# Two activation tiles begin 160 bytes off the grid of 512 bytes

## The chip, the core and the metric

The kernel runs on one core of one Trainium2 chip. The time is the device time of one execution in microseconds (us). A core has a matrix engine (TensorE, "PE" in the profile, its weight loads "PEld"), a vector engine (VectorE, "DVE"), a scalar engine (ScalarE, "ACT"), GpSimd ("POOL") and a queue engine that issues most of the transfers (SyncE, "SP"). All of them work on an on-chip memory of 128 partitions, in which a tile has the same byte address in each partition. TensorE multiplies two operands: one is loaded into the array as weights (128 x 128), the other is streamed through it, up to 512 columns at a time; the result is summed up in accumulator banks.

## The reference, cut to what matters

A trunk of two layers on 256 positions of width 2048. Both layers project their input, run a main branch and a four-head attention over 256 memory positions, gate both, project the result with `w_out`, and normalise.

```
h = x
for i in range(2):
    if i == 1:
        k_blocks, v_blocks, k_mean = moba_shared_kv(h, w_kv_shared)
    u = h @ w_in[i]                       # 2048 -> 4096 columns
    branch_in, gate_b, mem_q, gate_m = split(u)
    branch = multiscale_pool(...) if i == 0 else moba_attention(...)
    mem_o = memory_attention(mem_q, mem, w_mem_kv[i])
    mixed = concatenate([branch * silu(gate_b), mem_o * silu(gate_m)])
    h = layer_norm(ALPHA * h + mixed @ w_out[i], ln_g[i], ln_b[i])
```

All arithmetic is float32. Most of the work is the products of the 256 positions with the weights `w_in`, `w_out`, `w_mem_kv` and `w_kv_shared`.

## The kernel before, in words

To keep float32 accuracy at the fast matmul format, each operand is held as two tiles, a high part and a low part (`split`, L62 to L65: ScalarE writes the rounded high part, VectorE the difference), and a product is three terms: high by high, high by low, low by high. The activations lie transposed in three large tiles: `xT` (the input of a layer), `memT` (the memory) and `zT` (the gated branches), each with 16 k-blocks of 512 columns, 256 of the high part and 256 of the low part. Weights come in blocks of 128 x 1024 (512 KB): a transfer into one of four `raw` buffers, then a split into one of four pairs `wh`, `wl`. The blocks make one list, `items`; `run` walks it and prepares three blocks ahead, so the order of all engines is written out by the list and by `later`, which puts follow-up work some items behind. Nothing is planned by cost.

Two helpers consume the blocks. `proj_t` has the weights as the loaded side and streams xT or memT: for each 128 x 128 piece, the high weights meet all 512 columns of a k-block (high and low of the activation), and the low weights meet the 256 columns of the high part. So 512-wide and 256-wide matmuls alternate in pairs, and two accumulator halves are added at the end (`fold`). A list of 4 blocks has 16 k-blocks by two pieces, 32 pairs. `proj_n` has the activations as the loaded side (xT, memT or zT) and streams 512 columns of the weights: three 512-wide matmuls for each k-block and half of the positions. `proj_t` makes keys, queries, gates and the pooling input; `proj_n` makes values and the output projections.

The second layer's output projection is read in four column blocks. The last is "kept": its weights are split not into the four buffers but into xT and memT, which nobody reads any more, and are multiplied at the very end by `last`, with zT as the loaded side and the kept weights streamed. In the built program, xT begins at byte 1152 of a partition, memT at 33920, zT at 66688, the `raw` buffers at 115840, `wh` at 132224 and `wl` at 148608: all are 128 more than a multiple of 512, and all slices that matmuls take from them are whole multiples of 512 bytes further.

Of the kernel before, what the change touches and what calls it, by code (L numbers as in the profile page):

```python
# [12 lines left out]
F32R = mybir.dt.float32r  # L13
# [4 lines left out]
P = 128  # L18
T = 256
D = 2048  # L20
KT = D // P
# [10 lines left out]

BLK = 1024
RAW_BUFS = 4
W_BUFS = 4
LD = 4
LEAD = 3
LD0 = 8
# [4 lines left out]
def trunk(ctx: ExitStack, tc: tile.TileContext, a: dict, out: bass.AP):  # L43
    nc = tc.nc
    ctx.enter_context(tc.manual_schedule())
    sb = ctx.enter_context(tc.tile_pool(name="sb", bufs=1))
    ps = ctx.enter_context(tc.tile_pool(name="ps", bufs=1, space=bass.MemoryType.PSUM))


    xT = sb.tile([P, KT, 2 * T], F32R, name="xT")  # L50
    memT = sb.tile([P, KT, 2 * T], F32R, name="memT")
    zT = sb.tile([P, KT, 2 * T], F32R, name="zT")
    res = sb.tile([P, 2, D], F32, name="res")
    ident = mask = psc = eps_t = stats = None
# [4 lines left out]
    def mm(o, l, r, start, stop):  # L59
        nc.tensor.matmul(o, l, r, start=start, stop=stop)  # L60
# [9 lines left out]
    def collect(fn, *args):  # L70

        base = len(items)
        fn(*args)
        got = items[base:]
        del items[base:]
        return got

    def item(src, cols, consume=None, dst=None):
        items.append(dict(src=src, cols=cols, consume=consume, dst=dst, cuts=(0, cols)))

    events = defaultdict(list)
    now = [0]
# [4 lines left out]
    def load_piece(it, c0, c1):  # L87
        if "raw" not in it:
            it["raw"] = it.get("land") or sb.tile([P, BLK], F32, name="raw", bufs=RAW_BUFS)
        nc.sync.dma_start(it["raw"][:, c0:c1], it["src"][:, c0:c1])  # L90

    def load(it):
        for c0, c1 in zip(it["cuts"], it["cuts"][1:]):
            load_piece(it, c0, c1)

    def prep_piece(it, c0, c1):
# [7 lines left out]
        if "w" not in it:  # L104
            it["w"] = to or (sb.tile([P, BLK], F32R, name="wh", bufs=W_BUFS),
                             sb.tile([P, BLK], F32R, name="wl", bufs=W_BUFS))
        wh, wl = it["w"]
        split(wh[:, c0:c1], wl[:, c0:c1], raw)

    def prep(it):  # L110
        for c0, c1 in zip(it["cuts"], it["cuts"][1:]):
            prep_piece(it, c0, c1)

    def run():
# [12 lines left out]
        for i in range(n):  # L127
            now[0] = i
            if i + LP < n:
                prep(items[i + LP])  # L130
            if LD0 <= i + LD < n:
                load(items[i + LD])
            it = items[i]
# [14 lines left out]
    def proj_t(mov, wblk, done):  # L148


        acc = []

        def consume(kb):
            def go(wh, wl, k0=0, k1=4):
                if not acc:
                    acc.extend(ps.tile([P, 512], F32, name="acc", bufs=4) for _ in range(2))
                h = wh.rearrange("p (k n) -> p k n", n=256)
                l = wl.rearrange("p (k n) -> p k n", n=256)
                for n in range(2):
                    s = slice(n * P, (n + 1) * P)  # L160
                    for kk in range(k0, k1):
                        k = 4 * kb + kk
                        if k < KT - 1:
                            mm(acc[n], h[:, kk, s], mov[:, k], k == 0, False)
                        mm(acc[n][:, :T], l[:, kk, s], mov[:, k, :T], False, False)
                        if k == KT - 1:
                            mm(acc[n], h[:, kk, s], mov[:, k], False, True)
                    if kb == 3:
                        done(n, acc[n])
            return go  # L170
        for kb in range(4):
            item(wblk[kb], BLK, consume(kb))

    def proj_n(sta, wblk, done, korder=range(8), banks=("acc", "acc")):

        acc = []
        korder = list(korder)

        def consume(j, kb):
            def go(wh, wl):  # L180
                if j == 0:
                    acc.extend(ps.tile([P, 512], F32, name=b, bufs=4 if b == "acc" else 1) for b in banks)
                h = wh.rearrange("p (k n) -> p k n", n=512)
                l = wl.rearrange("p (k n) -> p k n", n=512)
                for t in range(2):
                    for kk in range(2):
                        k = 2 * kb + kk
                        xh = sta[:, k, t * P:(t + 1) * P]
                        xl = sta[:, k, T + t * P:T + (t + 1) * P]
                        first, last = j == 0 and kk == 0, j == 7 and kk == 1  # L190
                        mm(acc[t], xh, h[:, kk], first, False)
                        mm(acc[t], xh, l[:, kk], False, False)
                        mm(acc[t], xl, h[:, kk], False, last)
                    if j == 7:
                        done(t, acc[t])
            return go
        for j, kb in enumerate(korder):
            item(wblk[kb], BLK, consume(j, kb))
# [34 lines left out]
    def heads_tile(name):  # L233
        return sb.tile([P, 4, 2 * T], F32R, name=name)
# [202 lines left out]
    def fresh(key, make):  # L437

        tiles = []

        def g():
            if not tiles:
                tiles.append(make())
                st[key] = tiles[0]
            return tiles[0]
        return g
# [19 lines left out]
    def after(fn):  # L466

        it = items[-1]
        old = it["consume"]

        def go(*w):
            if old is not None:
                old(*w)
            fn()
        it["consume"] = go
# [16 lines left out]
    def load_act(t, src, kb):  # L492
        item(a[src][kb], BLK, None, ("act", t, kb))
# [138 lines left out]
    for grp in range(3):  # L632
        k = fresh("k", lambda: heads_tile("kk"))
# [44 lines left out]
    for j, it in enumerate(collect(out_1)):  # L678
        items.append(it)
        if j == 0:  # L680
            after(load_gb_rows)
        if j >= 8 and j % 2:
            kb = (j - 8) // 2
            w3 = [t[:, 2 * kb:2 * kb + 2].rearrange("p k n -> p (k n)") for t in (xT, memT)]
            item(a["w_out"][1, 3, kb], BLK, None, ("keep", *w3))


# [2 lines left out]
    for i in range(4):  # L690
        items[RAW_BUFS + i]["land"] = scr[:, i * BLK:(i + 1) * BLK]

# [9 lines left out]
    for n in range(4):  # L702
        gb = sb.tile([P, 2, 512], F32, name="raw", bufs=RAW_BUFS)
        for j, nm in enumerate(("ln_g", "ln_b")):
# [3 lines left out]
    def last(t, c0, c1):  # L708
        o = ps.tile([P, 512], F32, name="acc", bufs=4)[:, :c1 - c0]
        for k in range(KT):  # L710
            zh = zT[:, k, t * P:(t + 1) * P]
            zl = zT[:, k, T + t * P:T + (t + 1) * P]
            mm(o, zh, xT[:, k, c0:c1], k == 0, False)
            mm(o, zh, memT[:, k, c0:c1], False, False)
            mm(o, zl, xT[:, k, c0:c1], False, k == KT - 1)
        return o

    def add(t, c0, c1, o):
# [21 lines left out]
    def store(t, c0, c1):  # L740
        nc.sync.dma_start(out[t * P:(t + 1) * P, c0:c1], res[:, t, c0:c1])

    o = last(0, 0, 512)
    nc.vector.bn_aggr(m0, stats[:, 1, :3].rearrange("p a b -> p (a b)"))
    for n in (1, 2):
        times_g(n)
    add(0, 0, 512, o)
    norm_stats(0, 4)
    o = last(1, 0, 256)
    finish(0, 0, 1)  # L750
    add(1, 0, 256, o)
    finish(0, 2, 3)
    o = last(1, 256, 512)
# [85 lines left out]
```

## Time and profile before

| what | value |
|---|---|
| median of 3 runs | 829.35 us (828.19 to 829.77) |
| profiled execution | 829.05 us, span of its instructions 827.1 us |
| TensorE busy | 814.7 us, 98% of the span, 4436 matmuls |
| VectorE, ScalarE busy | 559.0 us (68%), 397.3 us (48%) |
| TensorE clock granted | 0.995 of full speed over the span |
| transfers | 159.13 MB, mean 192 GB/s |

In the profile, a group of instructions is named by source line, engine, operation and tiles, "out<-in". For a matmul, the tile behind the arrow that is written first is streamed and the second is loaded. L60 is the one line that issues all matmuls, so that groups are told apart by tiles. After the count come busy time, mean ns of one, and idle time of the engine ahead of it. Matmuls overlap: one takes longer from start to end than the distance to the next, so a pace is read from starts. The chain of waits lists the work that ended last, followed back from the end; a stretch of it has a start, a length and a count of instructions.

### The profile page before, as it was taken

How to read it: one execution, taken by the hardware profiler on the slowest of the kernel's cores; microseconds unless marked ns; L12 is line 12 of the kernel's file. 1: busy time of each engine (PE TensorE's matmuls, PEld its weight loads, DVE VectorE, ACT ScalarE, POOL GpSimd, SP SyncE). 2: the span in 40 equal slices, each digit the busy share in tenths (PEclk: the TensorE clock that was granted, in tenths of full speed). 3: DMA queues.
4: the chain of work that ended last, by engine and by line, in shares of the span. 5: the costliest groups of instructions: out<-in, count | busy, mean ns of one | idle time of the engine just before them, and what ended most of it. 6: DMA issues, size and time to landing. Idle time of an engine off the chain costs nothing.

```text
span 827.1 us, 11533 instructions
## 1 busy us (share of the span) xinstructions
PE 814.7 (98%) x4436; PEld 702.7 (85%) x4436; DVE 559.0 (68%) x793; ACT 397.3 (48%) x578; POOL 0.2 (0%) x4
## 2 busy tenths in 40 slices
PE   7999999999999999999999999999999999999996
PEld 6888888898888888888888888888888888888885
DVE  5686668657957555797667667566665667568746
ACT  6564545545545434445465445454554445545520
POOL 0000000000000000000000000000000000000000
PEclk9999999999999999999999999999999999999998
DMA  8976545556558655675544544645545554546742
GB/s 316 299 249 198 172 153 183 177 170 215 179 170 296 208 197 195 196 240 197 192 159 148 186 171 154 205 157 198 178 164 170 181 183 169 184 150 235 264 137 102
DMA packets 47163, 159.13 MB, mean 192 GB/s; under 512 B 5375, under 2 KB 7167, under 8 KB 46847
## 3 DMA queue, kind: packets, MB, share of 16 engines
q1 hardware_dynamic: 46080, 155.47, 56.0%
q10 hardware_dynamic: 1028, 2.93, 0.9%
q8 instruction: 34, 0.56, 0.3%
q14 instruction: 21, 0.17, 0.1%
HBM read 156.28 MB, written 2.10 MB: 191 GB/s over the span
## 4 chain that ended last, share of the span: by engine, by line
PE 94%; DVE 2%; DMA 2%; issue 1%; ACT 0%; DVEq 0%; SPq 0%; ACTq 0%
PE acc L60 85%; PE o L60 3%; PE s L60 2%; PE pt L60 2%; DMA raw<-in_w_out 1%; DVE wl L65 1%; PE pt L343 0%; ACT wh L64 0%; PE pt L293 0%; DVE memT L65 0%; DMA raw<-in_w_mk 0%; DVE res L376 0%; DVE stats L377 0%; DVE res L782 0%; PE o L618 0%
## 5 line engine op out<-in xcount | busy, mean ns | idle before, releaser
L65 DVE TENSOR_TENSOR wl<-raw,wh 128x1024 fp32r<-128x1024 f32 (+3 forms) x274 | 324.6, 1190 | 179.6 <-ACT wh L64 176.8
L60 PE MATMUL acc<-xT,wh 128*128 128x512 f32 x1216 | 426.9, 399 | 0.0
L64 ACT ACTIVATE wh<-raw 128x1024 fp32r<-128x1024 f32 (+3 forms) x274 | 281.4, 1030 | 220.0 <-PE acc L60 159.8
L60 PE MATMUL acc<-xT,wl 128*128 128x256 f32 x1216 | 328.8, 281 | 0.0
L60 PEld LDWEIGHTS acc<-xT,wh 128*128 128x128 f32 x1216 | 223.9, 188 | 47.0
L60 PEld LDWEIGHTS acc<-xT,wl 128*128 128x128 f32 x1216 | 229.5, 189 | 7.2 <-DVE wl L65 0.2
L60 PE MATMUL acc<-wh,zT 128*128 128x512 f32 x448 | 139.9, 390 | 0.0
L60 PEld LDWEIGHTS acc<-wh,zT 128*128 128x128 f32 x448 | 84.1, 188 | 17.2
L60 PE MATMUL acc<-wl,zT 128*128 128x512 f32 x224 | 87.3, 390 | 0.1
L60 PE MATMUL acc<-wh,xT 128*128 128x512 f32 x192 | 59.6, 389 | 0.0
L201 ACT ACTIVATE fold<-acc 128x256 f32<-128x256 f32 x72 | 27.6, 384 | 58.4 <-PE acc L60 58.3
L60 PE MATMUL acc<-memT,wh 128*128 128x512 f32 x128 | 47.9, 417 | 4.2 <-ACT wh L64 4.2
L60 PEld LDWEIGHTS acc<-wl,zT 128*128 128x128 f32 x224 | 42.1, 188 | 9.0 <-DVE wl L65 0.5
L60 PEld LDWEIGHTS acc<-wh,xT 128*128 128x128 f32 x192 | 36.0, 188 | 7.4
L60 PE MATMUL acc<-wl,xT 128*128 128x512 f32 x96 | 37.3, 389 | 0.0
L60 PE MATMUL acc<-memT,wl 128*128 128x256 f32 x128 | 36.0, 291 | 0.0
L60 PEld LDWEIGHTS acc<-memT,wh 128*128 128x128 f32 x128 | 25.0, 198 | 9.6 <-ACT wh L64 4.4
L202 DVE TENSOR_TENSOR fold<-acc,fold 128x256 f32<-128x256 f32 x72 | 29.6, 420 | 5.3 <-ACT fold L201 5.3
L64 ACT ACTIVATE zT<-zf 128x256 fp32r<-128x256 f32 x32 | 12.9, 415 | 39.7 <-DVE zf L263 35.5
L60 PEld LDWEIGHTS acc<-memT,wl 128*128 128x128 f32 x128 | 25.4, 198 | 1.3 <-DVE wl L65 0.5
L64 ACT ACTIVATE ph<-pt 128x384 fp32r<-128x384 f32 (+1 forms) x20 | 10.7, 534 | 22.7 <-PE pt L343 13.6
L60 PE MATMUL acc<-xT,zT 128*128 128x256 f32 (+1 forms) x96 | 21.5, 318 | 0.0
(132 smaller groups left out, 626.2 us busy)
## 6 DMA issues: line engine op xcount, KB each, us to landing
raw<-in_w_in SPq DMA_DIRECT2D x128, 512.0 KB, 3.4
raw<-in_w_out SPq DMA_DIRECT2D x64, 512.0 KB, 4.2
raw<-in_w_sk SPq DMA_DIRECT2D x24, 512.0 KB, 3.9
raw<-in_w_sv SPq DMA_DIRECT2D x24, 512.0 KB, 3.4
raw<-in_w_mv SPq DMA_DIRECT2D x14, 512.0 KB, 5.2
raw<-in_w_mk SPq DMA_DIRECT2D x12, 512.0 KB, 4.4
raw<-in_xT SPq DMA_DIRECT2D x4, 512.0 KB, 4.5
res<-in_x ACTq DMA_DIRECT2D x2, 1024.0 KB, 5.4
```

What stands on the lines that cost most here:

```text
L60: nc.tensor.matmul(o, l, r, start=start, stop=stop)
L64: nc.scalar.activation(hi, src, AF.Copy)
L65: nc.vector.tensor_sub(lo, src, f(hi))
L201: nc.scalar.activation(dst, acc[:, T:], AF.Copy)
L202: nc.vector.tensor_add(dst, acc[:, :T], dst)
```

## The change

xT and memT become two views of one tile `xm`, both shifted by 40 elements of 4 bytes. The tile is 128 elements (512 bytes) longer than the two were together, so that zT, the weights and everything after them move by one whole step of 512 bytes. The kept weights get views of their own that begin at the start of `xm`, unshifted, and `last` reads those.

```
+SHIFT = 40
-    xT = sb.tile([P, KT, 2 * T], F32R, name="xT")
-    memT = sb.tile([P, KT, 2 * T], F32R, name="memT")
+    xm = sb.tile([P, 2 * KT * 2 * T + 128], F32R, name="xm")
+    KX = KT * 2 * T
+    xT, memT = (xm[:, SHIFT + i * KX:SHIFT + (i + 1) * KX].rearrange("p (k t) -> p k t", k=KT) for i in range(2))
+    kept = [xm[:, i * KX:(i + 1) * KX].rearrange("p (k n) -> p k n", k=KT) for i in range(2)]
...
-            w3 = [t[:, 2 * kb:2 * kb + 2].rearrange("p k n -> p (k n)") for t in (xT, memT)]
+            w3 = [t[:, 2 * kb:2 * kb + 2].rearrange("p k n -> p (k n)") for t in kept]
...
-            mm(o, zh, xT[:, k, c0:c1], k == 0, False)
-            mm(o, zh, memT[:, k, c0:c1], False, False)
-            mm(o, zl, xT[:, k, c0:c1], False, k == KT - 1)
+            mm(o, zh, kept[0][:, k, c0:c1], k == 0, False)
+            mm(o, zh, kept[1][:, k, c0:c1], False, False)
+            mm(o, zl, kept[0][:, k, c0:c1], False, k == KT - 1)
```

More of the change, by code (lines that the diff above doesn't have):

```diff
@@ L34 @@
 RAW_BUFS = 4
+SHIFT = 40
 W_BUFS = 4
+SHIFT = 40
 LD = 4
```

## The prediction

> **What bounds the kernel.** I read the page's first part, then the chain of waits, then TensorE's own timeline at four places, because the change touches nothing but addresses and only the pace of single reads can answer it. First the page:
>
> ```profile
> span 827.1 us, 11533 instructions
> PE 814.7 (98%) x4436; PEld 702.7 (85%) x4436; DVE 559.0 (68%) x793; ACT 397.3 (48%) x578; POOL 0.2 (0%) x4
> PEclk9999999999999999999999999999999999999998
> PE 94%; DVE 2%; DMA 2%; issue 1%; ACT 0%; DVEq 0%; SPq 0%; ACTq 0%
> L60 PE MATMUL acc<-xT,wh 128*128 128x512 f32 x1216 | 426.9, 399 | 0.0
> L60 PE MATMUL acc<-xT,wl 128*128 128x256 f32 x1216 | 328.8, 281 | 0.0
> L60 PE MATMUL acc<-memT,wh 128*128 128x512 f32 x128 | 47.9, 417 | 4.2 <-ACT wh L64 4.2
> L60 PE MATMUL acc<-memT,wl 128*128 128x256 f32 x128 | 36.0, 291 | 0.0
> L60 PE MATMUL acc<-wh,xT 128*128 128x512 f32 x192 | 59.6, 389 | 0.0
> L60 PE MATMUL acc<-wl,xT 128*128 128x512 f32 x96 | 37.3, 389 | 0.0
> ```
>
> TensorE is busy 98% of the span and carries 94% of the chain that ended last. Idle time before the large groups is 0.0, so no producer, DMA or eviction sets their end; the pace at which matmuls follow each other does. The duration of one (399 ns) overlaps its neighbours, so the pace must be read from starts. In the names, the operand written first is the one that streams, the second the one that is loaded as weights: xT and memT stream in 2 x 1216 + 2 x 128 = 2688 matmuls (`proj_t`). They are the loaded side in 192 + 96 = 288 for xT and, by the rows of the tile memT (first to last start in us), in 192 for memT: 480 in all (`proj_n`).
>
> ```profile
> L60 PE MATMUL acc<-wh,memT x64: 389/393/481, 363.6 to 387.7; 128*128 128x512 f32 x64
> L60 PE MATMUL pt<-wh,memT x32: 389/389/396, 12.8 to 50.0; 128*128 128x512 f32 x32
> L60 PE MATMUL o<-wh,memT x32: 389/389/389, 14.2 to 51.4; 128*128 128x512 f32 x32
> L60 PE MATMUL acc<-wl,memT x32: 387/389/396, 364.0 to 387.5; 128*128 128x512 f32 x32
> L60 PE MATMUL pt<-wl,memT x16: 389/389/398, 13.1 to 49.8; 128*128 128x512 f32 x16
> L60 PE MATMUL o<-wl,memT x16: 389/389/389, 14.4 to 51.1; 128*128 128x512 f32 x16
> ```
>
> Now the pace at three kinds of place: columns are start and duration in us.
>
> ```profile
> 5.04 0.63 PE L60 MATMUL acc<-memT,wh 128*128 128x512 f32 x1
> 8.88 0.63 PE L60 MATMUL acc<-memT,wh 128*128 128x512 f32 x1
> ```
>
> ```profile
> 782.63 0.62 PE L60 MATMUL acc<-wh,zT 128*128 128x512 f32 x2
> 783.08 0.39 PE L60 MATMUL acc<-wl,zT 128*128 128x512 f32 x1
> 783.31 0.62 PE L60 MATMUL acc<-wh,zT 128*128 128x512 f32 x2
> 783.76 0.39 PE L60 MATMUL acc<-wl,zT 128*128 128x512 f32 x1
> 783.99 0.62 PE L60 MATMUL acc<-wh,zT 128*128 128x512 f32 x2
> 784.44 0.39 PE L60 MATMUL acc<-wl,zT 128*128 128x512 f32 x1
> 784.67 0.62 PE L60 MATMUL acc<-wh,zT 128*128 128x512 f32 x2
> ```
>
> ```profile
> 815.73 0.28 PE L60 MATMUL acc<-xT,zT 128*128 128x256 f32 x1
> 816.69 0.28 PE L60 MATMUL acc<-xT,zT 128*128 128x256 f32 x1
> ```
>
> The first fence lies before the clock is granted: six pairs of one 512-wide and one 256-wide matmul take 8.88 - 5.04 = 3.84 us, 640 ns a pair, which is 768 columns at 0.833 ns. At the granted clock I take twice that speed: 320 ns a pair, 213.3 and 106.7 ns for the single widths. But nine 512-wide matmuls take 784.67 - 782.63 = 2.04 us, 226.7 ns each, and the eight 256-wide ones between the last two rows take 0.96 us, 120 ns each. So at full clock every matmul pays 13.3 ns over its columns, and at half clock none. A cost that appears only when the array asks twice as fast lies on the side that supplies it, that is in reading the two operands; at half clock it hides. By the rates of equal neighbours, a mixed pair should take 226.7 + 120.0 = 346.7 ns. It does not:
>
> ```profile
> 78.62 11.31 PE acc L60 x64
> 414.97 11.31 PE acc L60 x64
> 490.17 11.16 PE acc L60 x64
> 586.09 11.16 PE acc L60 x64
> 682.01 11.16 PE acc L60 x64
> ```
>
> These are the stretches of the chain in which one item list of `proj_t` (32 pairs) runs unbroken: 11.31 / 32 = 353.4 ns or 11.16 / 32 = 348.8 ns a pair, mean of the five 11.22 / 32 = 350.6. The same instructions on equally placed tiles run at two paces, and closer up they do it in a pattern:
>
> ```profile
> 415.17 0.39 PE L60 MATMUL acc<-xT,wh 128*128 128x512 f32 x1
> 415.51 0.40 PE L60 MATMUL acc<-xT,wh 128*128 128x512 f32 x1
> 415.87 0.40 PE L60 MATMUL acc<-xT,wh 128*128 128x512 f32 x1
> 416.23 0.40 PE L60 MATMUL acc<-xT,wh 128*128 128x512 f32 x1
> ```
>
> One pair takes 0.34 us, the next two 0.36 each. Nothing waits there (idle 0.0), so the two reads of TensorE, the streamed tile and the weights of the next matmul, meet differently from pair to pair.
>
> **The change, part by part.** *What it adds and removes: nothing.* The built program has the same instructions in the same order on each engine, with the same semaphore waits and values; one tile in place of two brings no new dependence. DMA issues, buffers and queues are as before, and zT, weights and all later tiles move by 512 bytes, so that their places within 512 bytes are kept. *What moves:* in the built program all matmul operands begin at 128 past a multiple of 512 (xT 1152, memT 33920, zT 66688, the first `wh` 132224, the first `wl` 148608). After it xT and memT begin at 288 past one. All columns, k-blocks and halves are whole multiples of 512 bytes, so in the trace of before every streamed start and every weight start of the products agree modulo 512. Only the three correction matmuls at the very end, at half clock, load a tile that lies elsewhere. No row at full clock shows another offset, and the price has to be bounded from both sides.
>
> *The 2688 streamed reads.* The pair at 350.6 ns is the term. Upper bound of the gain: all pairs as short as the shortest shown, 340 ns: (350.6 - 340) x 1344 = 14.2 us. Upper bound of the loss: all as long as the longest of the pattern, 360 ns: (360 - 350.6) x 1344 = 12.6 us. Between them lie two natural resting places. All pairs at the sum of the even rates, 346.7: (350.6 - 346.7) x 1344 = 5.2 us, or, where the long pattern at 353.4 is the usual one, (353.4 - 346.7) x 1344 = 9.0 us. All pairs in the long pattern: 2.8 x 1344 = 3.8 us lost. I take the first, with the middle of 5.2 and 9.0: 7.1 us gained. My reason is that the mixed pair is the only place where the kernel runs above its own even rates, that this excess is a matter of how two reads fall on each other, and that the change parts precisely these two. This is a choice between near neighbours, not a proof: the pattern also changes with time alone while addresses agree, so time may decide it without address.
>
> *The 480 matmuls with xT or memT loaded as weights.* They run at the even 512-wide rate (389 ns durations, as for zT). Bound either way by half of the 13.3 ns: 480 x 6.7 = 3.2 us. I take 0, because this kind shows one pace and no second to fall into.
>
> *Writes of ScalarE and VectorE into the shifted tiles.*
>
> ```profile
> L64 ACT ACTIVATE xT<-raw x12: 1043/1062/1063, 26.8 to 789.2; 128x1024 fp32r<-128x1024 f32 x12
> L64 ACT ACTIVATE memT<-raw x5: 416/630/1061, 3.1 to 32.0; 128x256 fp32r<-128x256 f32 x2, 128x1024 fp32r<-128x1024 f32 x2, 128x512 fp32r<-128x512 f32 x1
> L64 ACT ACTIVATE wh<-raw 128x1024 fp32r<-128x1024 f32 x258 | 271.7, 1057 | 211.1 <-PE acc L60 156.3 <-issue 15.8 <-DMA raw<-in_w_out 11.3
> ```
>
> Columns of the tile's rows are count, shortest, median and longest ns, first and last start. Eight of the twelve writes to xT are kept weights and stay in place. ScalarE waits for TensorE 156 us in front of the weight splits; if each remaining write took a tenth longer, about 0.1 us of 1.06, that slack would hide it. The exception is the start, where the first memT splits (two of 256 columns, one of 512) stand ahead of the first matmuls with nothing to hide them: a tenth of 0.42 + 0.42 + 0.63 is 0.15 us. I take 0. *The last stage* reads kept weights against zT, both unshifted: 0. If TensorE runs faster in `proj_t`, the next thing late would be the weight split on VectorE, which is 68% busy over the span, so a 1% faster TensorE does not reach it.
>
> **Sum.** The profiled execution took 829.05 us, 1.95 us outside its span; the median of the runs is 829.35. 829.05 - 7.1 = 821.95; set on the median, 822.2 us.
>
> A page rule speaks against all this. The Trainium skill, "SBUF — State Buffer", section "Who interferes with whom", gives TensorE two independent read ports, one for the streamed operand and one for the weights, and says that TensorE waits for no other engine. By that rule the offset does nothing, 829.35. The trace does not agree that the reads are free of cost (13.3 ns per matmul at full clock and none at half), though it cannot say that the two reads are the reason.
>
> **Rivals.** *Nothing happens (829.35).* The 13.3 ns is a cost of each weight load wherever it lies, and the two patterns are a matter of time alone. For it: the same pace with xT, memT or zT as operand, and a pattern that changes without any address changing. Against it: only that the addresses have never been apart. It would be so at 0.6 ns or less per streamed matmul (1.66 us / 2688).
>
> *The other side: a split unit of reading (838).* 160 is a multiple of 32 but not of 64, and the old start, 128, is a multiple of both. If operands are read in units of 64 bytes or more, each streamed row and each loaded row now touches one unit more. At the step between the pair sum 346.7 and the long pattern, 6.7 ns a pair: 1344 x 6.7 = 9.0 us, 838.3; with the loads at 3.2 us more, 841.5. It decides from 0.6 ns per streamed matmul. For it: all reads are aligned today, a matmul is bound by supply, and there is no slack at full clock. Against it: nothing in the trace shows the size of a unit. A milder form, in which the shift merely holds all pairs in the long pattern, gives 833.
>
> *A larger gain (about 788).* If the two reads do collide and are wholly parted, a pair falls to 320: 30.6 x 1344 = 41.1 us. Against it: the even matmuls show 13.3 ns at both widths, as a fixed cost would.
>
> **How the numbers follow.** The measurement tells about 0.2% (1.7 us) from no change. Gain to the even rates or to 340: 0.40. Larger gain: 0.05. Nothing: 0.17. Slower by the long pattern or the split unit: 0.38, of which 0.10 lies over 841. Faster is then 0.45, same 0.17, slower 0.38. The range runs from all pairs at 340 (829.05 - 14.2, rounded to 814) to all at 360 without the loads (841). The forecast's own range is 814 to 826.
>
> **What will show it.** Right: unbroken stretches of 64 in the chain take 11.1 us or less each, pair starts are 0.347 us apart, and everything outside `proj_t` keeps its pace (226.7 and 120 ns). Rival of nothing: the same 11.31 and 11.16. Split unit: the 64 take 11.5 or more, or `proj_n` with xT loaded rises above 226.7 while zT stays there. Any change in the last stage or in ScalarE's writes would mean that I have missed what the shift touches.

## The result and the profile after

The changed kernel takes 825.27 us (median of 6 runs, 824.36 to 827.22) where the kernel before takes 828.55 (6 runs, the three shown above among them, 828.04 to 829.77): a ratio of 0.996, 95% interval 0.9947 to 0.9974. It is faster, by less than half of what was forecast. The profiled execution took 824.92 us against 829.05.

The page of the changed kernel, its parts on busy time and on the costliest groups; `xm` stands for xT, memT and the kept weights alike, and L66 is L60 of before:

```profile
span 823.0 us, 11533 instructions
PE 810.0 (98%) x4436; PEld 700.7 (85%) x4436; DVE 558.7 (68%) x793; ACT 397.1 (48%) x578; POOL 0.2 (0%) x4
L66 PE MATMUL acc<-xm,wh 128*128 128x512 f32 x1344 | 468.0, 395 | 4.8 <-ACT wh L70 4.5
L66 PE MATMUL acc<-xm,wl 128*128 128x256 f32 x1344 | 363.1, 280 | 0.1
L66 PE MATMUL acc<-wh,zT 128*128 128x512 f32 x448 | 139.9, 390 | 0.0
L66 PE MATMUL acc<-wh,xm 128*128 128x512 f32 x256 | 82.6, 398 | 0.0
```

Two rows of before beside them, with zT and with memT loaded:

```profile
L60 PE MATMUL acc<-wh,zT 128*128 128x512 f32 x448 | 139.9, 390 | 0.0
L60 PE MATMUL acc<-wh,memT 128*128 128x512 f32 x64 | 21.4, 400 | 0.0
```

TensorE is still busy 98% of the span, and its time is 4.7 us less (814.7 before). The group `wh,zT` is what it was, 139.9 us. The group `wh,xm` is not: 256 matmuls take 82.6 us, where before they took 59.6 (xT) and 21.4 (memT), 81.0 together. So one kind of work became cheaper and another dearer.

The chain of waits of the changed kernel (start, length, work), first the unbroken lists of 32 pairs in `proj_t`, then lists of `proj_n` with memT loaded:

```profile
78.19 11.12 PE acc L66 x64
411.71 11.12 PE acc L66 x64
485.89 11.12 PE acc L66 x64
581.87 11.12 PE acc L66 x64
677.85 11.12 PE acc L66 x64
...
12.53 1.39 PE pt L66 x6
13.92 1.40 PE o L66 x6
...
363.94 5.60 PE acc L66 x24
373.21 5.60 PE acc L66 x24
```

And the rows of before for the same `proj_n` lists:

```profile
13.00 1.37 PE pt L60 x6
14.37 1.36 PE o L60 x6
...
363.89 2.77 PE acc L60 x12
...
367.10 5.47 PE acc L60 x24
376.22 5.48 PE acc L60 x24
```

The five lists of pairs, 11.31 or 11.16 us before, are now all 11.12, 347.5 ns a pair: the second pace is gone. But 24 matmuls with memT loaded take 5.60 us instead of 5.47, and six take 1.40 instead of 1.36.

To compare kernels, I took from each trace the mean distance from one matmul's start to the next, at full clock, and left out distances in which the engine was interrupted (over 420 ns for a pair, more than 45 ns over its columns for a single one; pairs and their parts are filtered apart, so that the parts don't add up exactly). A stretch of matmuls of one width is called an even run from here on.

| | before | after |
|---|---|---|
| pair of `proj_t` (512 + 256 wide), ns | 351.7 | 347.6 |
| its 512-wide part, its 256-wide part, ns | 235.1, 116.8 | 229.8, 117.4 |
| `proj_n`, xT or memT loaded, ns | 227.3 | 233.2 |
| `proj_n`, zT loaded, ns | 227.0 | 227.0 |
| last stage, 512 and 256 wide, ns | 226.7, 119.9 | 226.7, 119.9 |

1344 pairs by 4.1 ns are 5.5 us gained, and 480 by 5.9 ns are 2.8 us lost: 2.7 us of the 4.1 by which the two profiled executions differ. Summed over all distances, `proj_t` with the half-clock start gives 6.6 us less (478.1 to 471.5), `proj_n` with xT or memT 2.8 more (109.7 to 112.4), everything else 0.3 less. Of the 1.1 us in `proj_t` beyond the whole pairs, 0.75 lie in the lists before the first `proj_n` (8.64 to 7.89 us): the profiled execution of before has seven pairs of 640 ns there, at the half clock, and that of the changed kernel three. In the run with a shift of 256 bytes below, whose paces are those of before, the same lists take 8.30 us, so that part of the 0.75 is the moment at which the clock rose and not the layout. The rest lies where lists join and was not followed further.

### The profile page after: what moved, and what is told of

It reads as the page before. It is cut to its first block, busy times and chain, and to the rows that moved or that the text cites. A ratio compares the mean times of both kernels' runs of the same rounds, so it can differ in the third digit from the quotient of the medians.

```text
span 823.0 us, 11533 instructions
## 1 busy us (share of the span) xinstructions
PE 810.0 (98%) x4436; PEld 700.7 (85%) x4436; DVE 558.7 (68%) x793; ACT 397.1 (48%) x578; POOL 0.2 (0%) x4
## 4 chain that ended last, share of the span: by engine, by line
PE 98%; DVE 1%; DMA 1%; SPq 0%; ACT 0%; issue 0%; DVEq 0%
PE acc L66 89%; PE o L66 4%; PE s L66 2%; PE pt L66 2%; DMA raw<-in_w_mk 1%; PE pt L350 0%; PE pt L300 0%; SPq L97 0%; DVE res L789 0%; PE pt L625 0%; PE o L625 0%; DVE res L770 0%; DVE wl L71 0%; ACT wh L70 0%; DVE stats L728 0%
## 5 line engine op out<-in xcount | busy, mean ns | idle before, releaser
L66 PE MATMUL acc<-xm,wh 128*128 128x512 f32 x1344 | 468.0, 395 | 4.8 <-ACT wh L70 4.5
L66 PE MATMUL acc<-xm,wl 128*128 128x256 f32 x1344 | 363.1, 280 | 0.1
L66 PEld LDWEIGHTS acc<-xm,wh 128*128 128x128 f32 x1344 | 247.9, 188 | 53.2 <-ACT wh L70 5.1
L66 PEld LDWEIGHTS acc<-xm,wl 128*128 128x128 f32 x1344 | 253.2, 188 | 7.8 <-DVE wl L71 0.8
L66 PE MATMUL acc<-wh,zT 128*128 128x512 f32 x448 | 139.9, 390 | 0.0
L66 PEld LDWEIGHTS acc<-wh,zT 128*128 128x128 f32 x448 | 84.1, 188 | 17.3
L66 PE MATMUL acc<-wl,zT 128*128 128x512 f32 x224 | 87.2, 389 | 0.0
L66 PE MATMUL acc<-wh,xm 128*128 128x512 f32 x256 | 82.6, 398 | 0.0
L66 PEld LDWEIGHTS acc<-wh,xm 128*128 128x128 f32 x256 | 48.1, 188 | 11.4
L66 PE MATMUL acc<-wl,xm 128*128 128x512 f32 x128 | 50.2, 392 | 0.0
L66 PEld LDWEIGHTS acc<-wl,zT 128*128 128x128 f32 x224 | 42.1, 188 | 8.5
L66 PEld LDWEIGHTS acc<-wl,xm 128*128 128x128 f32 x128 | 24.1, 188 | 5.4
L66 PE MATMUL acc<-xm,zT 128*128 128x256 f32 (+1 forms) x144 | 22.6, 318 | 0.0
L66 PEld LDWEIGHTS acc<-xm,zT 128*128 128x128 f32 x144 | 20.7, 190 | 1.9
```

## The experiments

The traces left two readings. *Theory R*: what counts is the distance of the streamed operand's start from the loaded one's, modulo some length. *Theory A*: what counts is each operand's own place, with 64 bytes as the unit. All kernels below do the same work; the ratios are against runs of the kernel before beside them, whose medians were 828.55 to 828.68 us.

### Everything shifted together

```
+    sb.tile([P, 40], F32, name="gap")
     xT = sb.tile([P, KT, 2 * T], F32R, name="xT")
     memT = sb.tile([P, KT, 2 * T], F32R, name="memT")
```

> Every matmul operand moves by the same 160 bytes, so that streamed and loaded tiles agree modulo 512 again, as in the kernel before, but none begins on a multiple of 64. Theory R (what counts is the distance of the streamed start from the loaded start, modulo 512): the paces of before, pairs of proj_t at 349 to 353 ns, proj_n at 226.7 ns with xT, memT and zT alike, time 828 to 829.5 us. Theory A (what counts is where each tile lies by itself: off a multiple of 64 a loaded tile costs 7 ns a matmul, and a streamed one ends the long pattern): pairs at 347 ns, every proj_n matmul at about 233.6 ns, zT's 672 too, 825.3 + 672 x 0.007 = about 830 us.

Measured: 828.53 us, ratio 1.0001 (0.9991 to 1.001). Pairs 351.8 ns, `proj_n` with xT or memT 227.3, with zT 227.0. The chain shows the two paces of before to the last digit:

```profile
78.80 11.31 PE acc L61 x64
415.15 11.31 PE acc L61 x64
490.35 11.16 PE acc L61 x64
586.27 11.16 PE acc L61 x64
682.19 11.16 PE acc L61 x64
```

All operands begin off a multiple of 64 here, and nothing changes. Theory A in this form falls; what is left of the change is the distance between the two operands.

### Other shifts

```
-SHIFT = 40
+SHIFT = 16
```

The constant counts elements of 4 bytes: 16 is 64 bytes. The others are 64 (256 bytes), 88 (352), 32 (128), 8 (32) and 4 (16).

> The shift is 64 bytes instead of 160: multiples of 64 everywhere, streamed and loaded starts apart. Theory A: nothing is off a multiple of 64, so the paces of before: pairs at 349 to 353 ns, all of proj_n at 226.7 ns, 828.5 us. Theory R: paces other than before in proj_t or in proj_n with xT and memT, how large is open; the time between 822 and 832 us.

> The shift is 256 bytes, half of 512, so the distance is the same seen from either operand, and all starts are multiples of 64. Theory A: the paces of before, 828.5 us. Theory R: the even 512-wide matmuls of proj_n with xT or memT loaded leave 226.7 ns, or the pairs of proj_t leave 349 to 353 ns; the two kinds see one distance, so they should move the same way.

> The shift is 352 = 512 - 160 bytes: proj_t now has the distance that proj_n has in the changed kernel, and the other way round. Theory R: proj_n with xT and memT at 226.7 ns or less, and the pairs of proj_t slower, by 7 ns for the 512-wide one at least: 347 + 7 = 354 ns or more, so 825.3 - 3.3 + 1344 x 0.007 = 831 us or more. Theory A (352 is off a multiple of 64 as 160 is): as the changed kernel, pairs 347 ns, proj_n 233.6 ns, 825.3 us.

> The distance between streamed and loaded starts counts (theory R); shifts of 0 and 256 bytes gave the same paces, 64, 160 and 352 did not. If it counts modulo 128, a shift of 128 is no shift: pairs 349 to 353 ns, proj_n 226.7 ns with xT and memT, 828.6 us. If modulo 256, 128 is the far side: proj_n with xT and memT over 226.7 ns, at about 233 ns as for the other shifts, so 828.6 + 480 x 0.0065 = 831.7 us with the pairs as before, or 825 with pairs at 347.

> 160 is 32 modulo 128, and 160 modulo 256. If the distance counts modulo 128, the shift of 32 bytes is the change itself: pairs 347 ns, proj_n with xT and memT 233 ns, stretches of 64 at 11.12 us, 825.3 us. If it counts modulo 256, 32 and 160 are different places, and one of the paces differs from those of the change.

> Half the smallest distance tried. If reads are told apart by units of 32 bytes or more, 16 bytes move each tile by half a unit: either as no shift (pairs 349 to 353, proj_n 226.7, 828.6 us) or, where a unit is then split, as the shift of 32 or slower in both kinds. If the unit is 16 bytes or less, the paces are new: proj_n over 226.7 ns as at every other distance but 0, pairs anywhere from 340 to 355.

| shift, bytes | pair of `proj_t`, ns | `proj_n`, xT or memT loaded, ns | time, us | ratio, 95% interval |
|---|---|---|---|---|
| 0 (before) | 351.7 | 227.3 | 828.6 | |
| 16 | 348.3 | 232.1 | 824.41 | 0.9946 (0.9931 to 0.996) |
| 32 | 347.6 | 233.3 | 825.22 | 0.9954 (0.9937 to 0.9971) |
| 64 | 351.9 | 233.3 | 830.56 | 1.0028 (1.0015 to 1.004) |
| 128 | 350.9 | 233.0 | 829.81 | 1.0012 (1.0003 to 1.0022) |
| 160 (the change) | 347.6 | 233.2 | 825.27 | 0.996 (0.9947 to 0.9974) |
| 256 | 351.8 | 227.4 | 828.45 | 0.9999 (0.999 to 1.0008) |
| 352 | 350.8 | 234.1 | 829.92 | 1.002 (1.001 to 1.0029) |

The lists of 32 pairs in the chains of waits for shifts of 256, 64 and 32 bytes, in that order, first and third of the five:

```profile
78.43 11.31 PE acc L66 x64
...
489.98 11.16 PE acc L66 x64
```

```profile
79.00 11.20 PE acc L66 x64
...
489.75 11.18 PE acc L66 x64
```

```profile
78.48 11.12 PE acc L66 x64
...
486.15 11.13 PE acc L66 x64
```

Three things follow. A shift of 256 bytes is no shift, in both kinds; a shift of 128 is one, since `proj_n` goes to 233.0. So of the lengths tried, the distance counts modulo 256. (160 and 32, which differ by 128, agree to 0.1 ns all the same; why is open.) In `proj_n`, every shift that was tried other than 0 and 256 costs 5 to 7 ns a matmul on average. The three long lists, 96 matmuls each with xT loaded, run at 226.7 ns at a shift of 0 or 256, at 233.3 at 16, 32, 64, 128 and 160, and at 234.1 at 352. At 16 the short lists with memT loaded have now the one pace and now the other:

```profile
12.65 1.36 PE pt L66 x6
...
363.69 5.60 PE acc L66 x24
...
369.73 2.73 PE acc L66 x12
```

In that kernel lists at the start run at 1.36 us for six, as in the kernel before, a later one at 5.60 for 24, as in the changed kernel, and the next at 2.73 for 12, 227.5 ns each, near the first pace again. The loaded tile is the same in all three, and so is the distance. In the pairs, some shifts help by 3 to 4 ns (16, 32, 160) and some help by less than 1 or not at all (64, 128, 352). Shifts that bring the loss without the gain are slower than before: the same kind of edit with 64 in place of 160 costs 0.28%.

The expectation for 256 under theory R missed: I had taken the length to be 512 and expected some change. So did the one for 352, which took the places of the two kinds to be exchanged: `proj_n` is not at 226.7 there but at 234.1, and the pairs are at 350.8, not at 354 or more. What a distance does to one kind doesn't carry over to the other. In `proj_n` the shifted tile is the loaded one, so a shift of 352 means a distance of -352 bytes there, which is 160 modulo 256; its pace of 234.1 ns comes back below, where other tiles have that distance. The expectation for 32 missed as well: if the distance counts modulo 256, one of the paces was to differ from those of the change, and none does. By itself that run would fit a count modulo 128, which the run with 128 bytes excludes.

### Letting the weights follow

If distance is all, the loss in `proj_n` must go when its weight blocks begin as far off as xT and memT. For that, a block's high and low part share a tile with 256 bytes to spare. (Two small tiles, `nb` and `sm`, give up unused columns to make room.)

```
+            if not to:
+                wp = sb.tile([P, 2 * BLK + 64], F32R, name="wp", bufs=W_BUFS)
+                off = it.get("off", 0)
+                to = [wp[:, off + i * BLK:off + (i + 1) * BLK] for i in range(2)]
+            it["w"] = to
...
             item(wblk[kb], BLK, consume(j, kb))          # in proj_n
+            items[-1]["off"] = 0 if sta is zT else SHIFT
```

> A control for the next three: the high and low part of a weight block lie in one tile of 2 x 1024 and 256 bytes more, so that a block can begin anywhere in it; here the shift is 0 everywhere. All theories: the paces of before (pairs 349 to 353 ns, proj_n 226.7 ns), 828.6 us; a buffer is now freed as one instead of as two, which the slack of ScalarE in front of its splits covers.

> The change, but the weight blocks of proj_n with xT or memT loaded begin 160 bytes later too, so that there the distance is 0 again; all others stay. Theory R: proj_n with xT and memT back at 226.7 to 227.3 ns, pairs at 347.6, so 825.3 - 480 x 0.006 = 822.4 us. If the 6 ns are a matter of the loaded tile's own place (theory A): proj_n stays at 233, 825.3 us.

> The same with 32 bytes. Theory R: pairs at 347.6 ns, proj_n at 227 ns with all three tiles, 822.3 us.

> The same with 16 bytes. Theory R: pairs at 348.3 ns, proj_n at 227 ns, 824.4 - 480 x 0.005 = 822 us; within 0.1% of the two above.

| | pair, ns | `proj_n`, xT or memT, ns | time, us | ratio, 95% interval |
|---|---|---|---|---|
| shift 0, shared tile | 351.7 | 227.4 | 828.69 | 1.0002 (0.9993 to 1.0011) |
| 160, weights follow | 347.6 | 227.7 | 822.90 | 0.9929 (0.9917 to 0.9941) |
| 32, weights follow | 347.6 | 227.0 | 822.19 | 0.9921 (0.9907 to 0.9934) |
| 16, weights follow | 348.3 | 232.8 | 825.39 | 0.9957 (0.9943 to 0.997) |

The shared tile costs nothing. With 160 and with 32 bytes the expectation holds. From the chain of the kernel with 32 bytes, the `proj_n` lists and one list of pairs:

```profile
13.79 1.36 PE o L66 x6
...
369.11 2.75 PE acc L66 x12
372.30 5.47 PE acc L66 x24
...
410.57 11.12 PE acc L66 x64
```

5.47 us for 24 matmuls is the pace of before, and 11.12 that of the changed kernel: gain without loss. This version is the fastest measured, 0.8% under the kernel before; its interval and that of 160 overlap.

With 16 bytes the expectation fails. Streamed and loaded starts agree there too, yet `proj_n` stays slow:

```profile
14.03 1.40 PE o L66 x6
15.43 1.40 PE pt L66 x6
16.83 1.40 PE o L66 x6
```

So distance is not all: with both operands 16 bytes further than before, the even run is slow, 233.3 ns in all long lists and 230 to 231 in the later short ones, although nothing parts the operands. Either a place counts by itself below 32 bytes, or the pace is settled by how a list is entered, as the two paces at one place and one distance in the kernel with the plain 16-byte shift suggest. The runs don't tell these apart.

### The exception undone

```
-    kept = [xm[:, i * KX:(i + 1) * KX].rearrange("p (k n) -> p k n", k=KT) for i in range(2)]
+    kept = [xT, memT]
```

> The change with its exception undone: the kept weights lie in the shifted tiles too, so the 144 matmuls of the last stage (48 of 512 columns, 96 of 256) stream at a distance of 160 from zT. If any distance but 0 (modulo 256) slows an even run, whichever operand is off, the 512-wide go from 226.7 to about 233 ns; the 256-wide from 119.9 by as much, if the cost is one per matmul: 144 x 0.0065 = 0.9 us, 826.2 us. If a shift of the streamed tile helps by itself, as it does in proj_t, both stay or fall and the time is 825.3 us or less.

Measured: 826.00 us, ratio 0.9964 (0.995 to 0.9978), which the time alone doesn't tell from the change. The trace does. TensorE's timeline of the last stage's 256-wide part, as much of it as falls into one window (so the counts differ), the changed kernel first, then this one:

```profile
804.80 8.20 PE L66 MATMUL acc<-xm,zT 128*128 128x256 f32 x67
```

```profile
804.73 8.61 PE L66 MATMUL acc<-xm,zT 128*128 128x256 f32 x72
```

Less the length of the last matmul (0.28), 7.92 us over 66 distances are 120.0 ns, and 8.33 over 71 are 117.3. The 512-wide part goes the other way, from 226.7 to 234.2 ns, beside the 234.1 of `proj_n` at a shift of 352: other tiles and other places, but the same distance of 160. So at a distance of 160, an even run of 512-wide matmuls loses 7.5 ns each and an even run of 256-wide ones gains 2.6, and the stage as a whole changes by 48 x 7.5 - 96 x 2.6 = 0.1 us. I had expected the 256-wide ones to lose as well, if the cost was one per matmul. The exception is worth next to nothing.

## Why the prediction was right, and where it was not

*What bounds the kernel.* Right. What changed is the pace of TensorE: ScalarE's and VectorE's busy times moved by 0.2 and 0.3 us, the instructions are the same, TensorE waits even 0.6 us longer at the start (4.8 us ahead of its first large group, 4.2 before), and the profiled execution still took 4.1 us less.

*The pairs.* The prediction said that all lists of 64 would take 11.1 us or less, with pairs at 347; they take 11.12 with pairs at 347.6. The size was set as the middle of 5.2 and 9.0, from the five lists; the mean over all pairs gives 351.7 - 347.6 = 4.1 ns, 5.5 us, near the lower of the two. Setting 7.1 overstated it by 1.6 us, because the usual pace before, 351.7, lay nearer to the mean of the five lists (350.6) than to the long pattern (353.4).

The reason that it gave for 347, that the pair would fall to the sum of the even rates, did not hold. At a distance of 160 the even rates are 234.2 (512 wide) and 117.3 (256 wide), as the last stage shows with the exception undone; their sum is 351.5, and the pair takes 347.6. The pair has a pace of its own. That it came out beside 346.7 is a coincidence of sizes. The second reason, that two reads of TensorE meet differently and that the change parts them, is borne out in one half: with all operands shifted alike by 160 bytes nothing changes, and shifting the two apart changes the pace of both kinds. So the distance counts. That two reads meet, and that a parting helps, is not shown; at 64 bytes the two are apart as well, and the pairs stay at 351.9. Nothing in the prediction told 160 from 64, so that the time fell at all owes something to the shift that was chosen: that part is luck.

*The 480 with xT or memT loaded.* This is the step that failed. It was taken at 0, "because this kind shows one pace and no second to fall into", with 3.2 us as the bound; it measured 480 x 5.9 = 2.8 us. One pace at one distance says nothing on other distances. Nor did the starts show quite one pace: the list of 12 with memT loaded at 363.89 us in the rows of before takes 2.77 us, 231 ns each, where the long lists with xT run at 226.7; only the durations were alike.

Together the two terms take the forecast gain of 7.1 us down to 7.1 - 1.6 - 2.8 = 2.7; measured are 828.55 - 825.27 = 3.3, and the 0.6 between them have no term. With the 480 at their bound of 3.2, the forecast would have been 825.4, close to the 825.27 measured, but partly by luck: the pairs gave 1.6 less than the middle, and the six runs of before lie 0.8 below the 829.35 on which the forecast was set. Letting the weights follow takes the loss away, as the forecast assumed it to be, and leaves 822.2 to 822.9 us. That this is the forecast's number is again helped by those 0.8: the gains are 6.4 and 5.7 us, not 7.1.

*The writes of ScalarE and VectorE and the last stage.* Taken at 0, and nothing speaks against it: the busy time of ScalarE is 397.1 us against 397.3, that of VectorE 558.7 against 559.0, and the last stage keeps 226.7 and 119.9.

*The rivals.* Nothing happens: out, since the interval ends at 0.9974 and both paces moved. The page rule that stood beside it (the Trainium skill, "SBUF — State Buffer", section "Who interferes with whom": two independent read ports, and TensorE waits for no one) doesn't describe what was measured: with the same instructions and only the distance of the two operands changed, an even run went from 227.3 to 233.2 ns a matmul. The split unit: its signature was half seen, `proj_n` with xT slower while zT stayed, but a unit of 64 bytes or more, that costs by each operand's own place, is refuted by two runs: at a shift of 64 bytes 64 divides all starts, and the kernel is slower; with everything shifted it divides none, and nothing changes. A unit of 32 bytes isn't refuted: it is one of the two readings left for 16 bytes with the weights following. A loss, as this rival had it, is what the edit gives with 64, 128 or 352 bytes. The larger gain: out.

What stays open is the mechanism. The runs give a table of paces by distance; they don't say why 16, 32 and 160 help the mixed pairs and 64 and 128 hardly do, nor what the two operands have in common that their distance counts.

## What to carry to other kernels

When one engine is busy throughout and hardly waits, compare its pace at equal instructions in different places: a second pace in the trace is work that no count of instructions shows. Where two operands are read at once, their distance is a parameter of the layout, and it has to be looked at for each pairing in which a tile takes part; a shift that serves a tile in one role can cost in the other, so let the partner follow. And one pace seen at one setting is no bound for another setting.

## What the runs showed of the hardware

- The pace of a matmul depends on the distance, modulo 256 bytes among the lengths tried, between the start of the streamed operand and that of the loaded one. With one of the two shifted, even runs 512 wide took a mean of 227.3 ns at 0 and 227.4 at 256 bytes, and 232.1 to 234.2 at all other shifts tried.
- It comes in steps: the long even lists run at 226.7, 233.3 or, at a distance of 160, 234.1 ns, and the lists of pairs of before at 11.31 or 11.16 us. Two steps can occur within one kernel, with the same instructions at the same distance.
- The sign depends on the run: at a distance of 160 bytes, even 256-wide matmuls go from 119.9 to 117.3 ns and mixed pairs from 351.7 to 347.6, while even 512-wide ones go up, from 226.7 to 234.2.
- At a distance of 0, shifting both operands by 160 or 32 bytes leaves the even 512-wide run at 227.7 and 227.0 ns; shifting both by 16 makes it 232.8.
